# Two-layer encoder in float32 on one core: half of the Strassen weight sums of the first MLP product made by accumulating DMA, and a fourth Strassen pair in the second

## The chip, the core and the metric

The kernel runs on one core of one Trainium2 chip. The metric is the device time of one execution in microseconds; lower is better. TensorE (PE) multiplies, VectorE (DVE) and ScalarE (ACT) prepare operands and take results out of PSUM, GpSimd (POOL) and SyncE (SP) mostly issue DMAs. Each engine runs its own list of instructions in order and waits on semaphores for the others.

## The reference

Two layers over 256 tokens of width 2048, all in float32. The attention half of a layer (latent attention and neighbourhood attention, gated and merged) is untouched by the change. The part that matters is the MLP:

```python
    h = rmsnorm(x, norm_mlp[l]) @ w_ff1[l]            # 2048 -> 8192
    x = x + jnp.square(jax.nn.relu(h)) @ w_ff2[l]     # 8192 -> 2048
```

## The kernel before

**Precision.** A float32 operand is split in two: `hi` is the value cast to the PE's float32r, `lo` is the rest. A product is three matmuls (hi by hi, lo by hi, hi by lo). For weights this split is made on the core: ACT casts (`L177`), DVE subtracts (`L178`). The function `cut` does it for a whole step, in the MLP in strips 2048 columns wide.

**Tiling.** `gemm_s` computes 256 rows by 1024 columns and walks over eight steps `j` of 256 rows of the weight. A step loads one weight tile `raw` of 128 partitions by 2048 (1 MB, `L449`, on SP's queue); three such buffers exist (`RBUFS`). A plain step takes eight products, that is 24 matmuls of 512 columns. A step in `pairs` uses Strassen's scheme in Winograd's form and takes seven products, 21 matmuls, for which it needs four sums of weight blocks (`L465` makes two in one instruction, 1024 wide; `L468` and `L469` one each, 512 wide) and four sums of activation blocks (`sums_of`, `L364` to `L367`). In a Strassen step `cut` then runs over 1536 columns of the raw weights and over the 2048 columns of the four sums, where a plain step has only the 2048 raw ones. The eight products collect in eight PSUM banks; after the last step DVE combines them (eight adds at `L477`, a copy on ACT at `L478`).

**The MLP.** It runs over four blocks `b` of 2048 hidden columns. In a block two calls of `gemm_s` make the first product (`g` = 0 and 1, weights `in_w_ff1`, Strassen steps `FIRST`). Their result goes through the squared ReLU, is transposed on PE (`turned_pair`, `L398`) and split again. Two calls then make the second product (weights `in_w_ff2`, Strassen steps `SECOND`); in the last block only one, the other half being plain matmuls (`gemm_a`). So a layer has eight calls of the first kind and seven of the second. In the first three blocks the second product is added to `xt` by four accumulating DMAs a call, issued from POOL (`L870`).

**Order.** The code is written step by step, but the order in which each engine's instructions stand comes from a scheduler that runs at build time. It moves work of one step ahead of another where buffers allow. Split weights have four `hi` and four `lo` buffers in the MLP (`HBUFS`), so DVE and ACT can be about two Strassen steps ahead of PE and no more.

Of the kernel before, what the change touches and what calls it, by code (L numbers as in the profile page):

```python
# [64 lines left out]
FIRST, SECOND = (2, 4, 6), (2, 4, 6)  # L65
# [10 lines left out]
def trunk(ctx: ExitStack, tc: tile.TileContext, x, w_in, w_uq, w_ukv, rpb, w_o_mla, w_o_na,  # L76
# [36 lines left out]
    cos_sb = const.tile([P, S], F32, name="cos_sb")  # L113
    sin_sb = const.tile([P, S], F32, name="sin_sb")
    turn = const.tile([P, P], F32, name="turn")
    half = const.tile([P, 2], F32, name="half")
    mask_sb = const.tile([P, GRID_W], F32, name="mask_sb")
# [192 lines left out]
    class Norm:  # L310
# [14 lines left out]
        def scales(self):  # L325
# [5 lines left out]
            v = keep.tile([P, 2], F32, tag="var", name="var", bufs=2)  # L331
# [27 lines left out]
    def sums_of(f):  # L359
# [3 lines left out]
        s1, s2, s3, s4 = (s[:, i * P:(i + 1) * P] for i in range(4))  # L363
        nc.vector.tensor_tensor(s1, a21, a22, op=ALU.add)  # L364
        nc.vector.tensor_tensor(s2, s1, a11, op=ALU.subtract)
# [1 line left out]
        nc.vector.tensor_tensor(s3, a21, a11, op=ALU.subtract)  # L367
# [47 lines left out]
    def gemm_s(w, c0, get, order, pairs, evac):  # L415
# [31 lines left out]
        for j in order:  # L447
            raw = raws.tile([P, 2048], F32, tag="raw", name="raw", bufs=RBUFS)
            nc.sync.dma_start(raw.rearrange("p (k n) -> p k n", n=1024),  # L449
                              w[2 * j * P:(2 * j + 2) * P, c0:c0 + 1024].rearrange("(k p) n -> p k n", p=P))  # L450
# [8 lines left out]
            if strips:  # L459
                whole_ts = wpool.tile([P, 2048], F32, tag="sums", name="sums", bufs=1)  # L460
# [498 lines left out]
```

## Time and profile before

Three runs gave 2616.14, 2615.67 and 12601.07 us; the median is 2616.14.

| | us |
|---|---|
| median of the runs | 2616.14 |
| profiled execution | 2616.59 |
| its span, first to last instruction | 2614.8 |
| ACT busy | 1483.6 (57%) |
| POOL busy | 101.2 (4%) |

The chain of work that ended last is PE for 88% of the span and instruction issue for 8%; DVE has 2% and ACT 1% of it. The granted TensorE clock is 0.999 of full speed, so throttling plays no part. DMA moved 508.95 MB, 195 GB/s in the mean.

To read the rows: a group gives its line, engine, operation, tiles and shapes, the count, the busy time in us, and the mean of one in ns. The table by stretches gives for each engine its busy time and, in brackets, how many instructions. In the timeline the first number is the start and the second the length in us. A matmul's row shows its whole passage through the array, and passages overlap, so what a matmul costs is the distance between starts.

### The profile page before, as it was taken

Reading aid. Unit: us, or ns where it says so; the run is one execution under the profiler, and the core shown is the slowest. Engines: PE = TensorE matmul, PEld = TensorE weight load, DVE = VectorE, ACT = ScalarE, POOL = GpSimd, SP = SyncE. Lnnn points to the kernel's source line nnn. Section 1 sums busy time; section 2 is a strip of 40 time slices with the busy share of each in tenths; the row PEclk is TensorE's granted clock in tenths of the full one; section 3 lists DMA queues with packets and bytes.
Section 4 is the critical chain, followed back from the end, with each engine's and each line's share of the span. In section 5 each row is a group of like instructions: output and inputs, shape, how many; then the busy total and the mean of one; then the engine's idle time right before and its main releaser. Section 6 shows DMA issues by size and latency. Waiting matters only on the chain.

```text
span 2614.8 us, 32295 instructions
## 1 busy us (share of the span) xinstructions
PE 2588.5 (99%) x12450; PEld 2173.8 (83%) x12450; DVE 2183.3 (83%) x2570; ACT 1483.6 (57%) x1737; POOL 101.2 (4%) x117
## 2 busy tenths in 40 slices
PE   8999999999999999999999999999999999999998
PEld 7888888888888888888888888888888888888886
DVE  6668789789998898988667787896999988988885
ACT  6555556556655656556545555564665556565563
POOL 1100000000000010000001000000000000100000
PEclk9999999999999999999999999999999999999999
DMA  7555555555566575675555555544556766856763
GB/s 243 184 160 187 199 193 162 162 192 192 196 210 224 193 236 194 207 236 189 180 192 177 167 186 193 194 160 161 194 178 211 235 197 194 247 194 209 234 194 129
DMA packets 175257, 508.95 MB, mean 195 GB/s; under 512 B 13696, under 2 KB 18176, under 8 KB 175104
## 3 DMA queue, kind: packets, MB, share of 16 engines
q1 hardware_dynamic: 166192, 490.08, 56.5%
q0 software_dynamic: 8768, 16.78, 3.3%
q8 instruction: 97, 1.59, 0.2%
q14 instruction: 56, 0.46, 0.1%
q10 hardware_dynamic: 144, 0.04, 0.0%
HBM read 492.18 MB, written 2.10 MB: 189 GB/s over the span
## 4 chain that ended last, share of the span: by engine, by line
PE 88%; issue 8%; DVE 2%; ACT 1%; DMA 0%; POOL 0%; SPq 0%; POOLq 0%; DVEq 0%; ACTq 0%
PE bank L428 59%; PE bank L244 8%; PE bank L279 7%; PE bank L248 4%; PE bank L283 3%; PE bank L223 2%; PE bank L398 1%; PE bank L224 1%; PE bank L252 1%; PE bank L254 1%; PE bank L253 1%; DVE lo L178 1%; PE bank L559 1%; PE bank L496 0%; ACT hi L177 0%
## 5 line engine op out<-in xcount | busy, mean ns | idle before, releaser
L428 PE MATMUL bank<-hi,pair 128*128 128x512 f32 x5124 | 1284.2, 390 | 4.1 <-ACT hi L177 3.9
L428 PEld LDWEIGHTS bank<-hi,pair 128*128 128x128 f32 x5124 | 958.0, 188 | 204.8 <-ACT hi L177 5.6
L178 DVE TENSOR_TENSOR lo<-raw,hi 128x2048 fp32r<-128x2048 f32 (+3 forms) x416 | 741.8, 1796 | 77.3 <-ACT hi L177 50.9
L177 ACT CAST hi<-raw 128x2048 fp32r<-128x2048 f32 (+3 forms) x416 | 622.8, 1517 | 307.5 <-PE bank L428 163.3
L428 PE MATMUL bank<-lo,pair 128*128 128x512 f32 x2562 | 697.6, 390 | 0.0
L428 PEld LDWEIGHTS bank<-lo,pair 128*128 128x128 f32 x2562 | 479.7, 188 | 99.3
L177 ACT CAST hi<-sums 128x2048 fp32r<-128x2048 f32 (+1 forms) x150 | 244.9, 1638 | 292.3 <-DVE sums L469 167.8
L178 DVE TENSOR_TENSOR lo<-sums,hi 128x2048 fp32r<-128x2048 f32 (+1 forms) x150 | 290.8, 1947 | 98.6 <-ACT hi L177 58.7
L202 DVE TENSOR_TENSOR lo<-raw,hi 128x1024 fp32r<-128x1024 f32 (+1 forms) x224 | 269.3, 1208 | 117.2 <-ACT hi L201 116.5
L201 ACT CAST hi<-raw 128x1024 fp32r<-128x1024 f32 (+1 forms) x224 | 230.6, 1036 | 217.7 <-PE bank L279 84.7
L244 PE MATMUL bank<-hi,pair 128*128 128x512 f32 x1024 | 261.0, 391 | 0.0
L244 PEld LDWEIGHTS bank<-hi,pair 128*128 128x128 f32 x1024 | 190.3, 188 | 38.2
L477 DVE TENSOR_TENSOR wide<-wide,bank 128x512 f32<-128x512 f32 x336 | 214.9, 679 | 6.5 <-PE bank L428 6.4
L279 PE MATMUL bank<-pair,hi 128*128 128x512 f32 x768 | 203.4, 397 | 4.3 <-ACT hi L201 3.1
L465 DVE TENSOR_TENSOR sums<-raw 128x1024 f32<-128x1024 f32 x126 | 153.6, 1219 | 6.2 <-DMA raw<-in_w_ff 4.8
L279 PEld LDWEIGHTS bank<-pair,hi 128*128 128x128 f32 x768 | 136.3, 190 | 26.8 <-ACT hi L201 3.5
L248 PE MATMUL bank<-lo,pair 128*128 128x512 f32 x512 | 141.6, 391 | 0.0
L283 PEld LDWEIGHTS bank<-pair,lo 128*128 128x128 f32 x768 | 106.9, 190 | 8.7
L248 PEld LDWEIGHTS bank<-lo,pair 128*128 128x128 f32 x512 | 95.6, 188 | 19.4
L283 PE MATMUL bank<-pair,lo 128*128 128x256 f32 x768 | 111.6, 283 | 0.0
L407 ACT CAST pair<-wide 128x512 fp32r<-128x512 f32 x110 | 68.2, 620 | 56.8 <-DVE wide L366 54.5
L469 DVE TENSOR_TENSOR sums<-raw,sums 128x512 f32<-128x512 f32 x126 | 86.6, 687 | 2.1
(131 smaller groups left out, 1727.3 us busy)
## 6 DMA issues: line engine op xcount, KB each, us to landing
raw<-in_w_ff SPq DMA_DIRECT2D x256, 1024.0 KB, 5.2
raw<-in_w_in SPq DMA_DIRECT2D x124, 1024.0 KB, 5.1
raw<-in_w_out SPq DMA_DIRECT2D x32, 1024.0 KB, 5.2
raw<-in_w_o_na SPq DMA_DIRECT2D x16, 1024.0 KB, 5.0
raw<-in_w_o_mla SPq DMA_DIRECT2D x16, 1024.0 KB, 5.0
xt<-wide POOLq DMA_DIRECT2D x48, 256.0 KB, 5.5
raw<-in_w_ukv SPq DMA_DIRECT2D x8, 1024.0 KB, 5.0
raw<-in_w_uq SPq DMA_DIRECT2D x8, 768.0 KB, 4.6
```

The costliest lines, as they stand in the source:

```text
L177: nc.scalar.copy(hi, src)
L178: nc.vector.tensor_tensor(lo, src, hi.bitcast(F32), op=ALU.subtract)
L201: nc.scalar.copy(hi, src)
L202: nc.vector.tensor_tensor(lo, src, hi.bitcast(F32), op=ALU.subtract)
L244: nc.tensor.matmul(ps[t], a, wh[:, k], start=k0 + k + i == 0, stop=False)
L248: nc.tensor.matmul(ps[t], sides(have(acts, k0 + k), t)[0], wl[:, k], start=False, stop=k0 + k == nk - 1)
L279: nc.tensor.matmul(ps[m], wh[:, k, m * P:(m + 1) * P], have(acts, k0 + k), start=k0 + k == 0, stop=False)
L283: nc.tensor.matmul(ps[m][:, :S], wl[:, k, m * P:(m + 1) * P], have(acts, k0 + k)[:, :S], start=False, stop=k0 + k == nk - 1)
L428: nc.tensor.matmul(b[i], x, y, start=count[i] == 1, stop=count[i] == total[i])
L465: nc.vector.tensor_tensor(ts[0].rearrange("p (a n) -> p a n", a=2), raw[:, :512].rearrange("p (a n) -> p a n", a=1).to_broadcast([P, 2, 512]),
L469: final = nc.vector.tensor_tensor(t4, raw[:, 1536:], t2, op=ALU.subtract)
L477: add = lambda o, a, c: nc.vector.tensor_tensor(o, a, c, op=ALU.add)
```

## The change

- `SECOND` goes from steps 2, 4, 6 to steps 2, 3, 5, 6: a fourth Strassen step in every `gemm_s` call of the second product.
- In the first product (`fed=True`) the sums t1 and t3 are no longer made on DVE at `L465`. Two DMAs on SP's queue load the two blocks that are not shared straight into a new tile `t13` (two buffers); when they have landed, one accumulating DMA from POOL adds the shared block, read twice, to both. `raw` is then loaded by two smaller DMAs without that block. t2 and t4 stay on DVE.
- To make this an addition, the signs of the sums are turned round: weight sums are now all additions, activation sums and the final combination take the subtractions. `sums_of` makes two of its four sums in one instruction.
- The one `sums` tile of 2048 columns in strips becomes `t13` (two buffers) and `t24` (one), each 1024 wide, and `cut` casts and subtracts each half by itself, into one `hi` and one `lo` tile.
- To make room for the second `t13`: the rotary and mask tables live in the attention half's pool and are loaded again in the second layer, and the outputs that nobody reads of the sum-of-squares activations go into tiles that are free anyway.

```diff
-FIRST, SECOND = (2, 4, 6), (2, 4, 6)
+FIRST, SECOND = (2, 4, 6), (2, 3, 5, 6)
...
-        def cut(src):
+        def cut(src, more=None):
             out, step = [], 2048 if strips else 1024
+            if more is not None:
+                hi, lo = (wpool.tile([P, 2048], F32R, tag=tag, name=tag, bufs=hbufs) for tag in ("hi", "lo"))
+                for c, v in ((0, src), (1024, more)):
+                    cs = slice(c, c + 1024)
+                    nc.scalar.copy(hi[:, cs], v)
+                    nc.vector.tensor_tensor(lo[:, cs], v, hi[:, cs].bitcast(F32), op=ALU.subtract)
+                return [(hi[:, i:i + 512], lo[:, i:i + 512]) for i in range(0, 2048, 512)]
...
-            nc.sync.dma_start(raw.rearrange("p (k n) -> p k n", n=1024),
-                              w[2 * j * P:(2 * j + 2) * P, c0:c0 + 1024].rearrange("(k p) n -> p k n", p=P))
+            src = w[2 * j * P:(2 * j + 2) * P, c0:c0 + 1024].rearrange("(k p) n -> p k n", p=P)
+            if fed and j in pairs:
+                t13 = wpool.tile([P, 1024], F32, tag="t13", name="t13", bufs=2)
+                fore, twice = (t13.rearrange("p (a n) -> p a n", a=2), src[:, 0:1, :512].to_broadcast([P, 2, 512]))
+                nc.sync.dma_start(t13[:, :512], src[:, 0, 512:])
+                nc.sync.dma_start(t13[:, 512:], src[:, 1, :512])
+                nc.gpsimd.dma_start(fore, twice, accum_op=ALU.add)
+                nc.sync.dma_start(raw[:, 512:1024], src[:, 0, 512:])
+                nc.sync.dma_start(raw[:, 1024:], src[:, 1])
+            else:
+                nc.sync.dma_start(raw.rearrange("p (k n) -> p k n", n=1024), src)
...
-                whole_ts = wpool.tile([P, 2048], F32, tag="sums", name="sums", bufs=1)
-                ts = whole_ts[:, :1024], whole_ts[:, 1024:]
+                if not (fed and j in pairs):
+                    t13 = wpool.tile([P, 1024], F32, tag="t13", name="t13", bufs=2)
+                ts = t13, wpool.tile([P, 1024], F32, tag="t24", name="t24", bufs=1)
...
-            nc.vector.tensor_tensor(ts[0].rearrange("p (a n) -> p a n", a=2),
-                                    raw[:, :512].rearrange("p (a n) -> p a n", a=1).to_broadcast([P, 2, 512]),
-                                    raw[:, 512:1536].rearrange("p (a n) -> p a n", a=2), op=ALU.subtract)
-            nc.vector.tensor_tensor(t2, raw[:, 1024:1536], t1, op=ALU.subtract)
-            final = nc.vector.tensor_tensor(t4, raw[:, 1536:], t2, op=ALU.subtract)
+            if not fed:
+                nc.vector.tensor_tensor(ts[0].rearrange("p (a n) -> p a n", a=2),
+                                        raw[:, :512].rearrange("p (a n) -> p a n", a=1).to_broadcast([P, 2, 512]),
+                                        raw[:, 512:1536].rearrange("p (a n) -> p a n", a=2), op=ALU.add)
+            nc.vector.tensor_tensor(t2, raw[:, 1024:1536], t1, op=ALU.add)
+            final = nc.vector.tensor_tensor(t4, raw[:, 1536:], t2, op=ALU.add)
...
-            w1, w3, w2, w4 = cut(whole_ts) if strips else cut(ts[0]) + cut(ts[1])
+            w1, w3, w2, w4 = cut(*ts) if strips else cut(ts[0]) + cut(ts[1])
...
+        if l:
+            tables()
...
-                gemm_s(w_ff1[l], b * D + g * 1024, lambda j: have(xg, j), range(8), FIRST, relu2)
+                gemm_s(w_ff1[l], b * D + g * 1024, lambda j: have(xg, j), range(8), FIRST, relu2, True)
```

The scheduler sets the order anew. Three places matter for what follows. The line numbers in the rows of the changed kernel are its own.

SP's queue at the start of the first product of the second block, before (one row a weight tile, steps 0 to 4):

```order
L449 DMA raw_7126<-in_w_ff1 128x2x1024
L449 DMA raw_7160<-in_w_ff1 128x2x1024
L449 DMA raw_7190<-in_w_ff1 128x2x1024
L449 DMA raw_7229<-in_w_ff1 128x2x1024
L449 DMA raw_7259<-in_w_ff1 128x2x1024
```

The same place now (`L461` and `L462` load a `t13`, `L464` and `L465` the rest of its `raw`), steps 0 to 5 and the `t13` of steps 2, 4 and 6:

```order
L467 DMA raw_7202<-in_w_ff1 128x2x1024
L461 DMA t13_7267<-in_w_ff1 128x512
L462 DMA t13_7267<-in_w_ff1 128x512
L467 DMA raw_7236<-in_w_ff1 128x2x1024
L461 DMA t13_7342<-in_w_ff1 128x512
L462 DMA t13_7342<-in_w_ff1 128x512
L464 DMA raw_7266<-in_w_ff1 128x512
L465 DMA raw_7266<-in_w_ff1 128x1024
L467 DMA raw_7311<-in_w_ff1 128x2x1024
L464 DMA raw_7341<-in_w_ff1 128x512
L465 DMA raw_7341<-in_w_ff1 128x1024
L467 DMA raw_7382<-in_w_ff1 128x2x1024
```

The `t13` of step 2 stands ahead of the weight tile of step 1, that of step 4 ahead of the tile of step 2; that of step 6 (`t13_7413`) comes right after these rows, since it takes the buffer that step 2 frees.

POOL's queue from the end of the second block to the third, before (the accumulating DMAs into `xt` of the two calls of the second product):

```order
L870 DMA xt0_87<-wide_8064 128x512
L870 DMA xt0_87<-wide_8066 128x512
L870 DMA xt1_88<-wide_8065 128x512
L870 DMA xt1_88<-wide_8067 128x512
L870 DMA xt0_87<-wide_8344 128x512
L870 DMA xt0_87<-wide_8346 128x512
```

The same place now (`L891` is the old `L870`, `L463` the accumulating DMA into a `t13`):

```order
L891 DMA xt0_82<-wide_8198 128x512
L891 DMA xt0_82<-wide_8200 128x512
L891 DMA xt1_83<-wide_8199 128x512
L891 DMA xt1_83<-wide_8201 128x512
L463 DMA t13_8577<-in_w_ff1 128x2x512
L463 DMA t13_8652<-in_w_ff1 128x2x512
L891 DMA xt0_82<-wide_8495 128x512
L891 DMA xt0_82<-wide_8497 128x512
L891 DMA xt1_83<-wide_8496 128x512
L891 DMA xt1_83<-wide_8498 128x512
L463 DMA t13_8723<-in_w_ff1 128x2x512
```

The first two accumulations of the next block stand between the two groups for `xt`, ahead of the group that waits for the end of the second product; only that of step 6 stands behind it.

DVE in the second product of the second block, first call, from step 4 (a Strassen step) to step 5, before:

```order
L465 TENSOR_TENSOR sums_7936<-raw_7934 128x1024
L178 TENSOR_TENSOR lo_7907<-raw_7904,hi_7906 128x2048
L468 TENSOR_TENSOR sums_7936<-raw_7934,sums_7936 128x512
L364 TENSOR_TENSOR wide_7764<-wide_7762 128x128
L367 TENSOR_TENSOR wide_7764<-wide_7762 128x128
L469 TENSOR_TENSOR sums_7936<-raw_7934,sums_7936 128x512
L365 TENSOR_TENSOR wide_7764<-wide_7764,wide_7762 128x128
L408 TENSOR_TENSOR pair_7770<-wide_7762,pair_7769 128x512
L178 TENSOR_TENSOR lo_7941<-raw_7934,hi_7940 128x1536
L366 TENSOR_TENSOR wide_7764<-wide_7762,wide_7764 128x128
L408 TENSOR_TENSOR pair_7774<-wide_7764,pair_7773 128x512
L178 TENSOR_TENSOR lo_7945<-sums_7936,hi_7944 128x2048
```

The same call now at step 3 (`raw_8024`), with sums of step 5 (`raw_8092`) between; `L484`, `L487` and `L488` are the old `L465`, `L468` and `L469`, `L176` is the old `L178` and `L447` its form for a half of the sums:

```order
L487 TENSOR_TENSOR t24_8027<-raw_8024,t13_8026 128x512
L484 TENSOR_TENSOR t13_8094<-raw_8092 128x1024
L488 TENSOR_TENSOR t24_8027<-raw_8024,t24_8027 128x512
L176 TENSOR_TENSOR lo_8032<-raw_8024,hi_8031 128x1536
L447 TENSOR_TENSOR lo_8036<-t13_8026,hi_8035 128x1024
L447 TENSOR_TENSOR lo_8036<-t24_8027,hi_8035 128x1024
L409 TENSOR_TENSOR pair_7884<-wide_7881,pair_7883 128x512
L487 TENSOR_TENSOR t24_8095<-raw_8092,t13_8094 128x512
L364 TENSOR_TENSOR wide_7898<-wide_7896 128x256
L409 TENSOR_TENSOR pair_7903<-wide_7896,pair_7902 128x512
L488 TENSOR_TENSOR t24_8095<-raw_8092,t24_8095 128x512
L367 TENSOR_TENSOR wide_7898<-wide_7898,wide_7896 128x128
```

What moved: the first sum of a Strassen step now stands a whole step earlier, and the subtraction on the sums is in two halves, the first of which needs only `t13`.

More of the change, by code (lines that the diff above doesn't have):

```diff
@@ L112, in trunk @@
     nc.scalar.dma_start(g_sb, gains)
[L113 to L117, printed above, removed]
+    const.tile([P, 8], F32, name="pad")
+    table = {}
     def tables():
-        for sb, src in ((mask_sb, mask), (cos_sb, cos), (sin_sb, sin), (turn, turns), (half, halves)):
-            nc.sync.dma_start(sb, src)
+        for name, src, width in (("mask", mask, GRID_W), ("cos", cos, S), ("sin", sin, S), ("turn", turns, P),
+                                 ("half", halves, 2)):
+            table[name] = tmp.tile([P, max(width, 64)], F32, tag=name, name=name, bufs=1)[:, :width]
+            nc.sync.dma_start(table[name], src)
     xt = [const.tile([P, D], F32, name=f"xt{t}") for t in range(2)]
@@ L305, in root @@
         nc.vector.tensor_scalar(v, v, 1.0 / width, EPS, op0=ALU.mult, op1=ALU.add)
-        col = keep.tile([P, 2], F32, tag="rcol", name=name, bufs=6)
+        col = keep.tile([P, 2], F32, tag="rcol", name=name, bufs=5)
         nc.gpsimd.tensor_tensor(col, v, mhalf, op=ALU.pow)
@@ L330, in scales @@
                                  start=True, stop=True)
-            v = keep.tile([P, 2], F32, tag="var", name="var", bufs=2)
+            v = keep.tile([P, 2], F32, tag="var", name="var", bufs=1)
             nc.vector.tensor_copy(v, ps[:, 0:4:2])
@@ L340, in __init__, with add @@
             self.sums = keep.tile([P, 2, 4], F32, tag="sums", name="sums", bufs=2)
-        def add(self, t, c4):
-            junk = keep.tile([P, 512], mybir.dt.bfloat16, tag="junk", name="junk", bufs=1)
+        def add(self, t, c4, junk=None):
+            if junk is None:
+                junk = small().bitcast(mybir.dt.bfloat16)
             nc.scalar.activation(junk, xt[t][:, c4 * 512:(c4 + 1) * 512], AF.Square,
@@ L347, in scale @@
         def scale(self):
-            v = keep.tile([P, 2], F32, tag="var", name="var", bufs=2)
+            v = keep.tile([P, 2], F32, tag="var", name="var", bufs=1)
             nc.vector.tensor_reduce(v, self.sums, axis=AX.X, op=ALU.add)
@@ L354, in scales @@
             self.scale()
-            self.half = keep.tile([P, 2], F32, tag="rcol", name="half", bufs=6)
+            self.half = keep.tile([P, 2], F32, tag="rcol", name="half", bufs=5)
             nc.vector.tensor_scalar_mul(self.half, self.col, 0.5)
@@ L362, in sums_of @@
         a11, a21, a12, a22 = (f[:, i * P:(i + 1) * P] for i in range(4))
[L363 to L365 removed]
+        s3, s1, s2, s4 = (s[:, i * P:(i + 1) * P] for i in range(4))
+        nc.vector.tensor_tensor(s[:, :2 * P].rearrange("p (a n) -> p a n", a=2),
+                                f.rearrange("p (a n) -> p a n", a=4)[:, 0:4:3],
+                                a21.rearrange("p (a n) -> p a n", a=1).to_broadcast([P, 2, P]), op=ALU.subtract)
+        nc.vector.tensor_tensor(s2, s1, a11, op=ALU.add)
         nc.vector.tensor_tensor(s4, a12, s2, op=ALU.subtract)
[L367 removed]
         return s
@@ L413, in turned_pair, with gemm_s @@
         yield
-    def gemm_s(w, c0, get, order, pairs, evac):
+    def gemm_s(w, c0, get, order, pairs, evac, fed=False):
         b, count, total = {}, {}, {i: 0 for i in range(1, 9)}
@@ L528, in rope @@
         pr = abank()[:, :S]
-        nc.tensor.matmul(pr, turn, t, start=True, stop=True)
+        nc.tensor.matmul(pr, table["turn"], t, start=True, stop=True)
         u = small()
-        nc.vector.tensor_tensor(u, pr, sin_sb, op=ALU.mult)
-        nc.vector.tensor_tensor(t, t, cos_sb, op=ALU.mult)
+        nc.vector.tensor_tensor(u, pr, table["sin"], op=ALU.mult)
+        nc.vector.tensor_tensor(t, t, table["cos"], op=ALU.mult)
         nc.vector.tensor_tensor(t, t, u, op=ALU.add)
@@ L622, in put @@
                 ke[e] = pair()
-                split(ke[e], t, half[:, e:e + 1])
+                split(ke[e], t, table["half"][:, e:e + 1])
         return put
```

25 lines of the change are left out of this document (13 added, 12 removed).

## Prediction

> **What bounds the kernel now.** I read the page's busy times first, then the waits of each engine, then the timeline of PE, then busy time by stretches of the MLP.
>
> ```profile
> span 2614.8 us, 32295 instructions
> PE 2588.5 (99%) x12450; PEld 2173.8 (83%) x12450; DVE 2183.3 (83%) x2570; ACT 1483.6 (57%) x1737; POOL 101.2 (4%) x117
> ```
>
> PE is busy for 99% of the span, but a matmul's row overlaps the next, so this alone does not show that PE never waits. The waits of PE and of SP's queue do:
>
> ```profile
> PE bank L428 <- ACT hi L177: 3.9, 4, 1.1
> PE bank L279 <- ACT hi L201: 3.1, 1, 3.1
> ...
> SPq L449 <- DVE lo L178: 1438.8, 296, 14.8
> ```
>
> In all 42 calls of `gemm_s` the matmuls of L428 waited 3.9 us, in four places. SP's queue waited 1438.8 us for DVE to free a weight buffer: loads come too early, not too late. Now PE's timeline in a call of the second product:
>
> ```profile
> 2214.60 4.70 PE L428 MATMUL bank<-hi,pair 128*128 128x512 f32 x20
> 2219.14 1.07 PE L428 MATMUL bank<-lo,pair 128*128 128x512 f32 x4
> ```
>
> Twenty matmuls start over 2219.14 - 2214.60 = 4.54 us: 227 ns each. A call has 3 x 21 + 5 x 24 = 183, so 41.5 us. The stretches below are first calls of the second product in the second layer's blocks 1 and 3, then the second call of block 3 and both calls of the first product in block 4 (columns: length, PE, PEld, DVE, ACT, POOL, clock, DMA share, GB/s):
>
> ```profile
> 2007.10:2050.40 43.30, 43.30 (x200) 35.96 (x199) 38.17 (x43) 26.77 (x26) 0.00 (x0) 1.00 0.57 182
> 2176.70:2220.00 43.30, 43.30 (x200) 35.96 (x199) 37.34 (x40) 26.78 (x25) 0.00 (x0) 1.00 0.52 162
> 2220.00:2261.50 41.50, 41.50 (x184) 34.35 (x184) 38.24 (x32) 21.33 (x13) 3.52 (x4) 1.00 0.87 269
> 2261.50:2303.00 41.50, 41.50 (x184) 34.35 (x183) 36.07 (x29) 21.53 (x13) 3.50 (x4) 1.00 0.73 226
> 2303.00:2346.30 43.30, 43.30 (x200) 35.92 (x199) 38.13 (x38) 26.47 (x25) 0.00 (x0) 1.00 0.55 186
> ```
>
> Calls last 41.5 us, or 43.3 where sixteen transposes fall in: their matmuls alone. In the MLP the number of matmuls sets the time. DVE follows at 37 to 38 of 43, so it is the next in line.
>
> **The change, part by part.** The prices:
>
> ```profile
> L428 PE MATMUL bank<-hi,pair 128*128 128x512 f32 x5124 | 1284.2, 390 | 4.1 <-ACT hi L177 3.9
> L178 DVE TENSOR_TENSOR lo<-raw,hi 128x2048 fp32r<-128x2048 f32 x186 | 423.7, 2286 | 48.4 <-ACT hi L177 35.6 <-PE bank L428 12.3
> L178 DVE TENSOR_TENSOR lo<-raw,hi 128x1536 fp32r<-128x1536 f32 x102 | 178.5, 1750 | 0.0
> L178 DVE TENSOR_TENSOR lo<-raw,hi 128x1024 fp32r<-128x1024 f32 x104 | 125.1, 1221 | 28.8 <-ACT hi L177 15.4 <-PE bank L428 11.8 <-issue 1.5
> L465 DVE TENSOR_TENSOR sums<-raw 128x1024 f32<-128x1024 f32 x126 | 153.6, 1219 | 6.2 <-DMA raw<-in_w_ff 4.8
> L469 DVE TENSOR_TENSOR sums<-raw,sums 128x512 f32<-128x512 f32 x126 | 86.6, 687 | 2.1
> L177 ACT CAST hi<-sums 128x2048 fp32r<-128x2048 f32 x102 | 195.4, 1915 | 246.7 <-DVE sums L469 167.8 <-PE bank L428 78.1 <-ACT wide L815 0.5
> L177 ACT CAST hi<-raw 128x1536 fp32r<-128x1536 f32 x102 | 151.3, 1483 | 119.7 <-DMA raw<-in_w_ff 65.9 <-PE bank L428 46.6 <-DMA raw<-in_w_out 6.4
> L177 ACT CAST hi<-raw 128x1024 fp32r<-128x1024 f32 x104 | 105.6, 1052 | 87.2 <-PE bank L428 44.8 <-PE bank L244 13.2 <-issue 12.7
> ```
>
> 1. *Fourth Strassen step in the second product.* Seven calls a layer, 14 in all, each 24 - 21 = 3 matmuls fewer: 42 x 227 ns = 9.53 us, all on the path, since PE is the path. By the Trainium skill (TensorE: Matmul & The Clock Gate, "Wait — 56ns, not 53.3ns?") warm matmuls of 512 columns start 215.7 ns apart, which would make it 9.06 us; the trace has 227 and decides.
>
> 2. *What that step costs DVE and ACT.* In place of one 2286 ns subtraction DVE has 1219 + 2 x 687 + 1750 + 2 x 1221 = 6785 ns, 4.5 us more by durations. Starts overlap by about 0.08 us an instruction, so some 4.1 us of time, in each of 14 calls: 57 us. ACT's casts grow by 1483 + 2 x 1052 - 1915 = 1.7 us a call, against 43.30 - 26.78 = 16.5 us idle. On the path: nothing where DVE has that much idle time ahead of PE's need, all of it where not. The margin is smallest late in the first call, where transposes and evacuation weigh on DVE too:
>
> ```profile
> 2206.87 1.91 ACT L177 CAST hi<-sums 128x2048 fp32r<-128x2048 f32 x1 [0.49 <-PE bank L428]
> 2210.52 1.98 PE L428 MATMUL bank<-hi,pair 128*128 128x512 f32 x8
> ...
> 2027.20 2.29 DVE L178 TENSOR_TENSOR lo<-sums,hi 128x2048 fp32r<-128x2048 f32 x1 [2.51 <-ACT hi L177]
> 2030.04 0.39 PE L428 MATMUL bank<-lo,pair 128*128 128x512 f32 x1
> ...
> DVE lo L178 <- ACT hi L177: 4.1, 3, 1.7
> ```
>
> The cast ended at 2208.78 and PE used it at 2210.52 (by the program's order): 1.74 us to spare. In the first block the subtraction ended at 2029.49 and was used at 2030.04: 0.55 us. If nothing else gave way, 4.1 us more on DVE and 0.7 us less on PE leave PE waiting 4.8 - 1.74 = 3.1 us in the six first calls of later blocks and 4.8 - 0.55 = 4.2 us in the two of first blocks: 27 us. That is the upper end; the lower is 0. But DVE idles 43.30 - 37.34 = 6.0 us in that call, 4.1 of it waiting for ACT (last row, for 2176.7 to 2220). The half-wise cast lets DVE begin after 1052 ns and not 1915, and the new order fills gaps with a sum of a later step. So 4.1 us have about 6.0 us of idle time to go into, nearly full: I take 0.25 us left in each of eight calls, 2.0 us, near the lower end. In the second calls the work comes to 38.24 + 4.1 = 42.3 us by durations against 40.8, but that call also catches up what the first left, and the call behind it falls by 3 x 1219 ns = 3.7 us: 0.
>
> 3. *Sums by DMA in the first product.* 48 Strassen steps lose 1219 ns each on DVE, 58.5 us. On the path nothing, since PE did not wait there; the time pays for item 2. The price is a chain: two loads, POOL, an accumulating DMA.
>
> ```profile
> raw<-in_w_ff SPq DMA_DIRECT2D x256, 1024.0 KB, 5.2
> xt<-wide POOLq DMA_DIRECT2D x48, 256.0 KB, 5.5
> ...
> L870 POOL DMA_DIRECT2D xt<-wide x48: 852/1151/1877, 760.4 to 2436.4; - x48
> ...
> DMA to landing us min/median/max: 3.2/5.5/8.9
> ...
> 2136.33 2.28 DVE L178 TENSOR_TENSOR lo<-sums,hi 128x2048 fp32r<-128x2048 f32 x1
> 2159.06 0.69 DVE L468 TENSOR_TENSOR sums<-raw,sums 128x512 f32<-128x512 f32 x1
> ...
> 2160.56 1.91 ACT L177 CAST hi<-sums 128x2048 fp32r<-128x2048 f32 x1 [1.89 <-DVE sums L469]
> 2166.51 3.34 PE L428 MATMUL bank<-hi,pair 128*128 128x512 f32 x14
> ```
>
> The old accumulating DMAs move 256 KB from SBUF; the new one 512 KB from HBM, a kind the trace lacks. Bounds: from 5.2 + 1.2 + 5.5 = 12 us to 5.2 + 1.9 + 2 x 8.9 = 25 us for the chain. The tightest is step 6, whose buffer comes free when step 2's sums are subtracted (2138.6) and whose sum DVE needs at 2159.06: 20.5 us. SP has nothing long ahead of it there, and POOL's four `xt` DMAs stand ahead of it in one call in four only. I take 15 us, nearer the lower end, since single such DMAs landed in 3.2 to 5.5 us: hidden, 0. At 25 us it is 4.5 us late. PE takes the cast sums after six matmuls on raw weights, at 2166.51 + 6 x 0.227 = 2167.87, and they were cast at 2162.47, so 0.9 us of lead would be left, and DVE's queue behind the late sum would use it up; I price that at about 1 us in each of 16 calls, 16 us. Where the chain is early nothing is gained either, since PE does not wait there.
>
> 4. *More traffic.* One step adds 0.26 MB of plain loads and 0.52 MB of accumulation.
>
> ```profile
> q1 hardware_dynamic: 166192, 490.08, 56.5%
> q0 software_dynamic: 8768, 16.78, 3.3%
> ```
>
> All engines' time per MB: 0.565 x 2614.8 / 490.08 = 3.0 us and 0.033 x 2614.8 / 16.78 = 5.1 us. So 0.8 + 2.7 = 3.5 us a step, 10.4 a call: the first product's shares go from 0.55 to 0.79 and from 0.73 to 0.98. Two steps' loads of that call start in the call before (0.87). Full, but loads have 1438.8 us of early waiting to eat up: 0, at worst part of item 3's 16 us.
>
> 5. *The rest.* `sums_of` in three instructions, turned signs, tables loaded again at the layer's border (0.35 MB behind three weight tiles that are there already) and unread outputs in other tiles: 0 between -1 and +1, by PE's few waits outside L428.
>
> Sum: 2616.59 (profiled execution, 0.45 above the median) - 9.53 + 2.0 = 2609.1 us. I predict 2609.
>
> **The rivals.**
> - *A: DVE runs out in the second product's first calls.* For it: margins of 1.74 and 0.55 us, and the four buffers, which stop DVE from carrying the time saved in the first product across. Against: 6.0 us idle in that very call. At full price 2616.6 - 9.5 + 27 = 2634, slower than before. It decides the sign from 9.5 / 8 = 1.2 us a call on.
> - *B: the accumulating DMA is late.* For it: an unknown kind of transfer, and DMA near its limit at a block's border. Against: 20.5 us of lead. 2609 + 16 = 2625.
> - *C: PE is not the bound and DVE is.* DVE's total rises: 28 sums of 687 ns, 14 x 1750, 232 x 1221, eight more activation splits of 0.7 us, less 34 x 1219, 14 x 2286 and 102 x 2289: about +27 us, so 2643. Against it stand 3.9 us of waits. By the Trainium skill (Perfetto Trace Analysis, "Identifying the Most-Contended Engine") matmul busy time is no measure, the weight loads' share is, and the engine with the highest share is the one to relieve; that would name DVE, 2183.3 against 2173.8 us. The even 227 ns between starts speak for PE.
> - *D: nothing is given back and the new order closes old gaps too:* 2605 or below.
>
> **Chances.** Forecast (2605.5 to 2613) 0.62; A (2613 to 2634) 0.19; B 0.10; C 0.04; D 0.05. The likeliest is the forecast, so 2609. For 8 in 10 I go from 2604, nearly all of D, to 2622, which holds half of A and most of B. Faster or slower by over 2%, about what a measurement of this kernel can tell from no change, means below 2564 or above 2668. Nothing here reaches the first: 0.01. The second takes A, B and C together: 0.03. Within: 0.96.
>
> **What would show it.** PE's matmuls at L429 (old L428) number 42 fewer, still 227 ns apart, with waits under 6 us: item 1 right. Second-product calls of 40.8 us (42.6 with transposes): right; calls longer by 1 us or more, with PE waiting for ACT hi or DVE lo: A. DVE waiting for a DMA into `t13`, landings over 10 us: B. DVE's busy time near 2210 us with an unchanged span: C. I am wrong if the time is over 2613, or if calls of the first product lengthen at all.

## The result and the profile after

| | before | after |
|---|---|---|
| median of the runs, us | 2616.3 | 2637.1 |
| span of the profiled execution, us | 2614.8 | 2637.4 |
| matmuls in the 42 calls of `gemm_s` (hi rows + lo rows) | 5124 + 2562 = 7686 | 5096 + 2548 = 7644 |

The changed kernel is slower: ratio 1.008, 95% interval 1.0068 to 1.0092 (further down, too, the brackets behind a ratio are this interval). The prediction was 2609, 2604 to 2622. 42 matmuls went and the span grew by 22.6 us, so PE waits some 32 us more than before. The engines' row and the waits, of the changed kernel:

```profile
span 2637.4 us, 32886 instructions
PE 2595.5 (98%) x12408; PEld 2160.0 (82%) x12408; DVE 2196.5 (83%) x2684; ACT 1515.9 (57%) x1875; POOL 154.4 (6%) x165
...
ACT hi L175 <- DMA raw<-in_w_ff: 169.0, 72, 5.8
...
ACT hi L446 <- DVE t L488: 99.3, 58, 5.2
...
DVE t L487 <- DMA t<-in_w_ff: 44.0, 6, 8.8
...
PE bank L429 <- ACT hi L175: 7.6, 10, 1.3
PE bank L429 <- DVE wide L496: 7.0, 10, 1.2
```

PE's waits are short and many: ten for a cast of weights, ten for a bank that DVE has not yet emptied. These two rows hold 14.6 of the 32 us; PE's weight loads wait for the same two, 14.4 and 14.3 us, and these waits may overlap with the others. The long waits lie one step back. ACT waits 169.0 us for weight tiles (74.7 before), and DVE waits 44.0 us for a sum made by DMA, in just six places, one in each first call (`g` = 0) of the first product in blocks 1 to 3 of the two layers (blocks are counted from 0 here, as in the code). Four successive calls, from the second product of one block into the first product of the next (columns: length, PE, PEld, DVE, ACT, POOL, clock, DMA share, GB/s):

```profile
2192.90:2235.50 42.60, 42.60 (x197) 35.35 (x196) 40.98 (x46) 27.41 (x29) 0.00 (x0) 1.00 0.52 169
2235.50:2277.10 41.60, 41.12 (x181) 33.63 (x180) 38.39 (x37) 22.35 (x17) 4.75 (x5) 1.00 0.78 230
2277.10:2319.30 42.20, 42.13 (x185) 33.98 (x183) 32.08 (x29) 20.31 (x15) 7.26 (x8) 1.00 1.02 308
2319.30:2364.00 44.70, 43.69 (x200) 35.94 (x200) 39.24 (x42) 30.58 (x31) 2.30 (x2) 1.00 0.74 235
```

The first has the 42.6 us that its three fewer matmuls should give (43.3 - 0.68). In the third DMA is full, and DVE, relieved of its sums, works only 32 of 42 us: it waits. The fourth lasts 44.7 us where it took 43.3.

To see all calls at once I took from each trace the time between the first matmuls of successive calls, less that of the same call before, plus 0.68 us (3 x 227 ns) where a call has a fourth Strassen step. What is left is what the call lost. It is summed below over the calls of a kind, in us; "first" is the first MLP call of a layer, and in the last column, a layer's last call (taken from its first matmul to its last), some loss is an exchange with the plain matmuls that run beside it. "Feeding" is short for the sums by DMA, and a call that has them is fed.

| kernel | first (2) | 1st product, g=0 (6) | 1st product, g=1 (8) | 2nd product, g=0 (6) | 2nd product, g=1 (6) | last (2) | median, us |
|---|---|---|---|---|---|---|---|
| changed | 0.2 | 7.5 | 9.3 | 6.4 | 4.4 | 7.8 | 2637.1 |
| e1 feeding, three steps | 0.2 | 0.5 | 1.4 | 2.9 | 0.0 | -1.8 | 2621.6 |
| e2 four steps, no feeding | 10.1 | 0.0 | 0.5 | 11.7 | 0.0 | 3.2 | 2635.4 |
| e3 no accumulation | 0.2 | 2.7 | 0.3 | 3.4 | 2.7 | 5.4 | 2615.2 |
| e4 two steps of three fed | 0.9 | 10.2 | 4.5 | 19.8 | 3.1 | 6.9 | 2650.7 |
| e5 four steps in g=1, no feeding | 11.2 | 0.0 | 0.5 | 0.1 | 0.0 | 0.0 | 2626.6 |
| e6 four steps, g=1 fed | 10.4 | 2.8 | 0.2 | 3.9 | 0.6 | 5.9 | 2630.5 |
| e7 plain DMA for the accumulating | 0.2 | 0.4 | 2.1 | 6.1 | 1.4 | 8.1 | 2621.8 |
| e8 four steps in g=1, all fed | 0.2 | 0.1 | 2.9 | 8.0 | 0.0 | 6.3 | 2631.4 |
| e9 before, four steps in g=1 | 0.0 | 0.0 | -0.1 | 0.9 | 1.8 | -1.8 | 2615.1 |
| e10 as e5, first call fed | 0.2 | 0.0 | 0.3 | 0.0 | 0.0 | 0.1 | 2614.7 |
| e11 as e6, block 0 fed too | 0.2 | 2.9 | 0.3 | 4.1 | 2.8 | 5.5 | 2618.9 |
| e12 no `xt` DMA from g=1 | 0.2 | 8.6 | 4.5 | 3.3 | 1.1 | 6.0 | 2630.4 |
| e13 four steps in g=0, all fed | 0.2 | 0.5 | 5.6 | 3.5 | 0.5 | 7.0 | 2626.0 |

### The profile page after: what moved, and what is told of

Same layout as the page of the kernel before. It is cut to its first block, busy times and chain, and to the rows that moved or that the text cites. A ratio compares the mean times of both kernels' runs of the same rounds, so it can differ in the third digit from the quotient of the medians.

```text
span 2637.4 us, 32886 instructions
## 1 busy us (share of the span) xinstructions
PE 2595.5 (98%) x12408; PEld 2160.0 (82%) x12408; DVE 2196.5 (83%) x2684; ACT 1515.9 (57%) x1875; POOL 154.4 (6%) x165
## 4 chain that ended last, share of the span: by engine, by line
PE 66%; DMA 13%; DVE 12%; issue 7%; ACT 1%; SPq 0%; POOL 0%; DVEq 0%; POOLq 0%; ACTq 0%
PE bank L429 37%; DMA raw<-in_w_ff 9%; PE bank L242 8%; PE bank L277 7%; DVE lo L176 6%; DMA t<-in_w_ff 4%; PE bank L246 4%; PE bank L281 3%; DVE lo L447 2%; PE bank L221 2%; DVE wide L496 1%; PE bank L399 1%; PE bank L222 1%; DVE t L487 1%; PE bank L250 1%
## 5 line engine op out<-in xcount | busy, mean ns | idle before, releaser
L429 PE MATMUL bank<-hi,pair 128*128 128x512 f32 x5096 | 1303.2, 391 | 17.4 <-ACT hi L175 7.6
L429 PEld LDWEIGHTS bank<-hi,pair 128*128 128x128 f32 x5096 | 949.7, 188 | 234.2 <-ACT hi L175 14.4
L175 ACT CAST hi<-raw 128x2048 fp32r<-128x2048 f32 (+3 forms) x416 | 615.1, 1501 | 364.4 <-DMA raw<-in_w_ff 169.0
L176 DVE TENSOR_TENSOR lo<-raw,hi 128x2048 fp32r<-128x2048 f32 (+3 forms) x416 | 733.6, 1778 | 61.1 <-ACT hi L175 43.2
L429 PE MATMUL bank<-lo,pair 128*128 128x512 f32 x2548 | 716.3, 391 | 1.1 <-DVE lo L447 0.8
L446 ACT CAST hi<-t 128x1024 fp32r<-128x1024 f32 x232 | 239.6, 1049 | 186.1 <-DVE t L488 99.3
L447 DVE TENSOR_TENSOR lo<-t,hi 128x1024 fp32r<-128x1024 f32 x232 | 276.4, 1219 | 16.2 <-PE bank L429 14.5
L242 PE MATMUL bank<-hi,pair 128*128 128x512 f32 x1024 | 261.7, 391 | 0.0
L496 DVE TENSOR_TENSOR wide<-wide,bank 128x512 f32<-128x512 f32 x252 | 165.5, 680 | 7.5 <-PE bank L429 7.4
L246 PE MATMUL bank<-lo,pair 128*128 128x512 f32 x512 | 143.3, 391 | 0.0
L463 POOL DMA_DIRECT2D t<-in_w_ff x48 | 58.2, 1212 | 1277.6 <-DMA t<-in_w_ff 680.2
L487 DVE TENSOR_TENSOR t<-raw,t 128x512 f32<-128x512 f32 x116 | 79.6, 686 | 63.5 <-DMA t<-in_w_ff 44.0
L484 DVE TENSOR_TENSOR t<-raw 128x1024 f32<-128x1024 f32 x68 | 83.1, 1223 | 30.9 <-DMA raw<-in_w_ff 30.6
```

The lines of the kernel that those rows point to most:

```text
L175: nc.scalar.copy(hi, src)
L176: nc.vector.tensor_tensor(lo, src, hi.bitcast(F32), op=ALU.subtract)
L242: nc.tensor.matmul(ps[t], a, wh[:, k], start=k0 + k + i == 0, stop=False)
L246: nc.tensor.matmul(ps[t], sides(have(acts, k0 + k), t)[0], wl[:, k], start=False, stop=k0 + k == nk - 1)
L429: nc.tensor.matmul(b[i], x, y, start=count[i] == 1, stop=count[i] == total[i])
L446: nc.scalar.copy(hi[:, cs], v)
```

## The experiments

Each starts from the changed kernel, but for e9. T1 and T2 in the first expectations are two theories: the loss comes from the DMA side, or from the fourth step's lack of time on DVE and ACT.

**e1, feeding alone.**

```diff
-FIRST, SECOND = (2, 4, 6), (2, 3, 5, 6)
+FIRST, SECOND = (2, 4, 6), (2, 4, 6)
```

> The changed kernel with three Strassen steps in the second product (2, 4, 6) as before; the sums by DMA in the first product stay. 42 matmuls more than the changed kernel. Theory T1, the loss comes from the DMA side (DMA engines full in the first product, the chain of step 6 late, the lateness handed on): the loss stays without the fourth step, about 2616 + 15 = 2628 to 2634 us. Theory T2, the loss comes from the fourth step, for which DVE and ACT have no room in the second product: 2614 to 2619 us, no slower than the kernel before.

2621.6 us, ratio 1.0016 (1.0007 to 1.0026), between the ranges of the two theories. The sums by DMA, together with the small edits of item 5, cost 5 us without the fourth step, although DMA is nearly as full as in the changed kernel (shares of 0.95 to 1.00 in the first calls of blocks 1 to 3, against 0.99 to 1.03). The three calls across a border:

```profile
1098.40:1139.80 41.40, 41.40 (x184) 34.32 (x183) 36.75 (x33) 23.23 (x18) 5.95 (x6) 1.00 0.97 295
1139.80:1181.30 41.50, 41.50 (x184) 34.36 (x183) 32.62 (x30) 20.33 (x16) 7.22 (x7) 1.00 0.97 283
1181.30:1224.60 43.30, 43.30 (x200) 35.93 (x199) 36.84 (x39) 27.80 (x29) 1.21 (x1) 1.00 0.68 213
```

PE is busy throughout. A nearly full DMA alone does not stop it. The other difference to the changed kernel is in the first row: 0.97 against 0.78, that is, loads for the next block run early.

**e2, the fourth step alone.**

```diff
-                gemm_s(w_ff1[l], b * D + g * 1024, lambda j: have(xg, j), range(8), FIRST, relu2, True)
+                gemm_s(w_ff1[l], b * D + g * 1024, lambda j: have(xg, j), range(8), FIRST, relu2)
```

> The changed kernel with all sums of the first product back on DVE (no feeding by DMA); the fourth step in the second product stays. T1: the first product goes back to 41.5 and 43.3 us a call, and only small losses are left in the second: 2607 to 2613 us. T2: DVE has 58 us more work than in the changed kernel and as little room in the second product, so the calls of the second product lose 1.2 us or more each: 2622 us or more.

2635.4 us, ratio 1.007 (1.0055 to 1.0085), in T2's range, with no accumulation into a `t13` anywhere. But all second calls take 40.8 us and so lose nothing, against T2; the first calls of the second product lose 11.7 us and the last ones 3.2. DVE and PE in such a first call:

```profile
1080.21 1.22 DVE L484 TENSOR_TENSOR t<-raw 128x1024 f32<-128x1024 f32 x1 [0.33 <-DMA raw<-in_w_ff]
1081.35 2.28 DVE L176 TENSOR_TENSOR lo<-raw,hi 128x2048 fp32r<-128x2048 f32 x1
...
1083.69 2.11 PE L429 MATMUL bank<-lo,pair 128*128 128x512 f32 x8 [0.74 <-DVE lo L176]
```

PE starts when the subtraction of 1081.35 ends. Ahead of that stood the first sum of a step that comes later, which itself waited 0.33 us for its load. Idle time of DVE was there, but not ahead of the work that was late. This is one wait of 0.74 us; that the others are of the same kind is not shown. The other 10 us, in a layer's first MLP call, are taken up in e5.

**e3, without the accumulating DMA; `t13` is used as loaded.**

```diff
-                nc.gpsimd.dma_start(fore, twice, accum_op=ALU.add)
```

> The changed kernel without the accumulating DMA: t13 is loaded and used as it is, so the shared block is left out of t1 and t3. PE, DVE and ACT do the same instructions; 25 MB of accumulating traffic and the second half of the chain are gone. T1: the DMA share in the first calls falls from about 1.0 to about 0.8, the first product is at 41.5 and 43.3 us a call again: 2607 to 2613 us. T2: nothing changes in the second product; what goes is at most the lengthening of the first product's calls: 2618 to 2628 us.

2615.2 us, ratio 0.9996 (0.9987 to 1.0006): between the two. Against the changed kernel 22 us, so that is the price of the accumulation beside four steps; e1 has it at 5 at most beside three. Against e2, 20 us less: DVE's relief is worth something, half of it in a layer's first call. The first calls of the second product lose 3.4 us in place of 11.7.

**e4, steps 2 and 4 fed, step 6 summed on DVE.**

```diff
+            by_dma = fed and j in pairs and j != 6
...
-            if fed and j in pairs:
+            if by_dma:
...
-                if not (fed and j in pairs):
+                if not by_dma:
...
-            if not fed:
+            if not by_dma:
```

> The changed kernel with steps 2 and 4 of the first product fed by DMA and step 6 back on DVE; four Strassen steps in the second product stay. T1: a third of the added traffic goes, and with it the step whose chain comes last; the first product loses less than half of what it loses now: 2612 to 2622 us. T2: DVE has 20 us more work, the second product loses what it lost: 2632 to 2642 us.

2650.7 us, ratio 1.0129 (1.0114 to 1.0144): worse than either theory has it. The late `t13` of step 6 is gone, but a weight tile is late in its place. The same two lines (`L487` and `L484` there) wait 18.2 and 30.6 us in the changed kernel; in e4:

```profile
DVE t L488 <- DMA raw<-in_w_ff: 49.3, 12, 6.6
DVE t L485 <- DMA raw<-in_w_ff: 41.8, 53, 1.8
```

So step 6's accumulation into the recycled `t13` buffer is not needed for a loss of this size. DMA is still at 1.00 to 1.02 in those calls. That the first calls of the second product lose 19.8 us was not taken apart further: the scheduler gave this kernel an order of its own.

**e5, the fourth step only in the second calls, no feeding** (with e2's edit).

```diff
-                gemm_s(w2, g * 1024, lambda j: have(hid, j), range(8), SECOND, residual2)
+                gemm_s(w2, g * 1024, lambda j: have(hid, j), range(8), SECOND if g else (2, 3, 6), residual2)
```

> No feeding; the fourth Strassen step stands only in the second calls of the second product (steps 2, 3, 5, 6), the first calls have three (2, 3, 6): 6 x 3 matmuls fewer than before, 18 x 227 ns = 4.1 us. In the run with pairs alone all six second calls lasted 40.80 us, so they lost nothing, and the first calls lost 1.3 to 3.1 us each. Theory 'the fourth step fits where no transposes and no evacuation of the first product fall in': 2616.6 - 4.1 = 2612.5, so 2611 to 2614.5, second calls 40.8 us, first calls 43.3. Rival 'the second calls only pass their lack of DVE time on': 2615 to 2622, with first-product calls or first calls of the second product longer than before.

2626.6 us, ratio 1.0038 (1.0025 to 1.0051), above both ranges. Of 30 MLP calls 28 lose next to nothing, as the theory says; all of the loss, 11.2 us, is in the first MLP call of each layer, where neither theory had it. DVE and PE there:

```profile
645.36 1.22 DVE L447 TENSOR_TENSOR lo<-t,hi 128x1024 fp32r<-128x1024 f32 x1
646.50 2.29 DVE L176 TENSOR_TENSOR lo<-raw,hi 128x2048 fp32r<-128x2048 f32 x1
648.70 1.22 DVE L484 TENSOR_TENSOR t<-raw 128x1024 f32<-128x1024 f32 x1
649.83 0.29 DVE L368 TENSOR_TENSOR wide<-wide 128x128 f32<-128x128 f32 x1
...
650.15 0.62 ACT L408 CAST pair<-wide 128x512 fp32r<-128x512 f32 x1 [3.44 <-DVE wide L368]
...
650.82 0.50 PE L429 MATMUL bank<-hi,pair 128*128 128x512 f32 x1 [3.33 <-ACT pair L408]
```

An activation sum of 0.29 us stands behind 4.7 us of weight work (1.22 + 2.29 + 1.22); ACT waits for it and PE for ACT. That is the order, not a lack of time. The 3.3 us are followed by a slower clock (last section).

**e6, four steps; only the second calls of the first product fed** (`relu2, g == 1)` for `relu2, True)`).

> Four Strassen steps in the second product as in the changed kernel; sums by DMA only in the second call of the first product. Theory 'DMA is full in the first call of the first product, because weight buffers come free late in the call before and the accumulations fall on top': the 7.5 us lost in those calls and most of the 4.4 us lost in the calls before go, DMA share there 0.75 to 0.9 instead of 1.0: 2622 to 2629. Rival 'every accumulating DMA costs its own delay on the chain wherever it stands': half of the 21 us that the accumulation costs goes, but DVE has half of its relief less, which gives about 5 us back: 2629 to 2635. Rival 'DVE's total decides': 2634 to 2638.

2630.5 us, ratio 1.005 (1.0034 to 1.0066), in the first rival's range, but 10.4 us of it is e5's stall, since the layer's first call is not fed either. Without it some 2620, below the first theory's range. The calls after it do as the first theory says: 0.2 us lost in g=1 in place of 9.3, 2.8 in g=0 in place of 7.5.

**e7, a plain DMA in place of the accumulating one, same queue, tile and waits.**

```diff
-                nc.gpsimd.dma_start(fore, twice, accum_op=ALU.add)
+                nc.gpsimd.dma_start(fore, twice)
```

> The changed kernel with a plain DMA in place of the accumulating one, same queue, same source, same tile, same waits: t13 then holds the shared block twice, so t1 and t3 lack the other block. The chain of two loads, POOL, DMA stays; only the kind of the transfer changes (by the profile of before 3.0 us of all engines per MB in place of 5.1, so 0.52 x 2.1 = 1.1 us a step, 3.3 us a call). Theory 'the accumulation's traffic costs the time': 2618 to 2627. Rival 'the length of the chain costs it': 2632 to 2638, within 5 us of the changed kernel.

2621.8 us, ratio 1.0021 (1.0012 to 1.0031), in the range of the traffic theory: the kind of the transfer is worth 15 us. A plain transfer with the same chain costs 6.6 us against e3. Rows of e7, then of the changed kernel:

```profile
q0 software_dynamic: 15680, 41.95, 5.9%
t<-in_w_ff POOLq DMA_DIRECT2D x48, 512.0 KB, 6.0
```

```profile
q0 software_dynamic: 21824, 41.95, 8.8%
t<-in_w_ff POOLq DMA_DIRECT2D x48, 512.0 KB, 9.2
```

Same bytes, 77 us less time of all engines (0.088 x 2637.4 - 0.059 x 2620.3), and 3.2 us less from issue to landing. The chain is shorter too, and DVE waits 27.0 us for `t13` in place of 44.0, so this run does not tell traffic from length.

**e8, all of the first product fed, the fourth step only in the second calls** (e5's edit alone).

> Sums by DMA in the whole first product; the fourth Strassen step only in the second calls of the second product (18 matmuls fewer than before). Theory 'DVE lacks time in the first calls alone': feeding alone took 2621.6, so 2621.6 - 4.1 = 2617.5, 2616 to 2619.5. Rival 'the fourth step in the second call holds the weight buffers longer, so that the loads of the next first product start late and meet the accumulations': second calls move 230 GB/s instead of 295 and first-product calls lose 1 to 2 us each: 2622 to 2630.

2631.4 us, ratio 1.0057 (1.0041 to 1.0073), above both ranges: 18 matmuls fewer than e1 and 9.8 us slower. The second calls take 40.8 us and lose nothing themselves; they move 256 to 259 GB/s, between the rival's 230 and 295. DVE waits 42.1 us for `t13`, again in six places, all in first calls of the first product. These lose 0.1 us, and the loss shows in later calls: 2.9, 8.0 and 6.3 us.

**e9, the kernel before with e5's edit of the steps and `SECOND` = 2, 3, 5, 6; e10, e5 with only the first MLP call of a layer fed** (`b == g == 0` for `True`).

> The kernel before (its sums, its tiles, no feeding) with a fourth Strassen step in the second calls of the second product alone (steps 2, 3, 5, 6 there, steps 2, 3, 6 in the first calls): 18 matmuls fewer, 4.1 us. Theory 'the fourth step fits into the second calls, and the 5 us lost in the first MLP call of a layer in three runs come from the order that the changed code got there': 2612.5, 2611 to 2614, all second calls 40.8 us, first MLP call of a layer 44.0 us. Rival 'the loss in a layer's first MLP call comes with the fourth step's activation sums': 2620 to 2625, that call 49 us.

> Fourth step in the second calls only, sums by DMA only in the very first MLP call of each layer (3 of 48 sums a layer... 6 in all). Theory 'that call stalls 5 us because DVE's sums stand ahead of an activation sum that PE waits for': with the sums off DVE there the call is back at 44.1 us, and 2626.6 less 11.2 gives 2615.4: 2613.5 to 2617. Rival 'the stall moves to another call': 2620 to 2628.

2615.1 us, ratio 0.9992 (0.9983 to 1.0001), and 2614.7, ratio 0.999 (0.9981 to 1.0). e10 is back at 44.1 us in the layer's first call, so e5's stall is the order around DVE's sums there; e9 never had it, so it does not come with the fourth step. e10 lies in its range, e9 1 us above its own. Both are some 2 us above the 2612.5 that 18 matmuls fewer would give: e9 loses 0.9 us twice in second calls, and in e10 the stretches outside the MLP are 1.5 and 1.0 us longer. These are the best versions, about 2 us under the kernel before (2616.9 beside them), at the edge of what the runs can tell.

**e11, four steps, fed everywhere except in the first calls (g = 0) of blocks 1 to 3** (`g == 1 or b == 0` for `True`).

> Four Strassen steps in all calls of the second product; sums by DMA everywhere in the first product except in the first calls (g = 0) of blocks 1 to 3, where the `xt` accumulations and the tail of the second product meet them. Theory 'the loss needs the accumulations in just those calls, since DVE enters them late and the sum of step 6 then comes behind its need': 2637.1 less 18 to 13 us, 2618 to 2624, no wait of DVE on a DMA into t13 over 2 us. Rival 'the loss is spread over all calls with accumulations': 36 of 48 sums remain, so 2630 to 2636.

2618.9 us, ratio 1.0007 (0.9998 to 1.0016), as the theory has it. (Six calls hold 18 of the 48 fed steps, so 30 remain, not the 36 that the rival counts; the rival's sum would then lie near 2637.1 - 18/48 x 22 = 2629, still far off.) Not feeding these six calls gives back 18 of the 28 us by which the prediction missed. DVE no longer waits for `t13` at all. The border of the same block as in e1, now:

```profile
1093.50:1136.00 42.50, 41.90 (x181) 33.48 (x180) 38.75 (x37) 22.19 (x17) 3.50 (x4) 1.00 0.72 217
1136.00:1178.30 42.30, 42.09 (x185) 34.20 (x184) 38.63 (x35) 22.97 (x17) 5.87 (x6) 1.00 0.92 292
1178.30:1221.60 43.30, 43.30 (x200) 35.96 (x199) 38.73 (x43) 28.47 (x29) 1.22 (x1) 1.00 0.73 225
```

**e12, without the accumulating DMAs into `xt` from the second calls of blocks 0 to 2.**

```diff
+                            if b < NB - 1 and g:
+                                continue
                             if b < NB - 1:
```

> The changed kernel without the accumulating DMAs into xt from the second calls of blocks 0 to 2 (that half of the second product is not added). This takes 1 MB of accumulation, by the profile of before 5.1 us of all DMA engines, out of each first call of the first product, and four issues off POOL's queue ahead of the sum of step 6; the chain of that sum (buffer free, two loads, POOL, accumulation) stays. Theory 'DMA is full there, traffic sets the pace': DMA share there 0.85 to 0.9, 2620 to 2628. Rival 'the buffer of step 6 comes free too late and the chain is too long': DVE still waits 4 us or more for that sum in each of the six calls, 2630 to 2637.

2630.4 us, ratio 1.0051 (1.0037 to 1.0064), at the lower edge of the rival, yet not for its reason. The wait for `t13` is down, and the wait for weight tiles is up:

```profile
DVE t L487 <- DMA raw<-in_w_ff: 46.2, 14, 6.1
...
DVE t L487 <- DMA t<-in_w_ff: 7.2, 4, 3.4
```

The DMA share there is 0.93 to 0.97, not 0.87, and the core still moves some 300 GB/s in those calls, as in the changed kernel: plain loads took the place of what was left out.

**e13, all of the first product fed, the fourth step only in the first calls** (`(2, 3, 6) if g else SECOND`).

> Sums by DMA in the whole first product as in the changed kernel; the fourth Strassen step only in the first calls of the second product (and the single call of the last block), three in the second calls: 24 matmuls fewer than before, 5.4 us. Theory 'with four steps in the second call DVE has no time to get ahead of PE before the next block begins, and only that lead hid the accumulations': with three steps there it gets ahead again, first calls of the first product last 41.5 us, DVE waits under 10 us in all for a DMA into t13, second-call DMA share 0.95 as with feeding alone; feeding alone 2621.6 less 5.4 plus 0 to 6 us of the loss in the first calls gives 2616 to 2622. Rival 'full DMA is enough, lead or not': the first product's calls lose 1 to 2 us each as in the changed kernel, 2628 to 2634.

2626.0 us, ratio 1.0036 (1.0022 to 1.005), between the two. The first calls of the first product are whole again (0.5 us lost), as the theory says, but so are e8's (0.1), which have four steps ahead of them. The calls after them still lose 5.6 us, and DVE still waits 34.9 us for `t13`, not the 10 at most of the theory.

## Why the prediction was wrong

**What failed first: item 3, the 20.5 us of lead, from which "hidden, 0" follows.** It weighs most, since 22 of the 28 us go with the accumulation (e3). The lead is the time from step 2's buffer coming free to DVE needing step 6's sum. It was called the tightest, but it was read in a second call of the first product (g = 1, from 2133.4). All six waits came in first calls (g = 0), and these had less already in the profile before. DVE in the one from 2091.9:

```profile
2096.94 2.28 DVE L178 TENSOR_TENSOR lo<-sums,hi 128x2048 fp32r<-128x2048 f32 x1
...
2112.59 0.69 DVE L468 TENSOR_TENSOR sums<-raw,sums 128x512 f32<-128x512 f32 x1
```

The buffer comes free at 2099.22, 7.3 us into the call, and step 6's sum begins at 2112.59: a lead of 13.4 us, in all six of these calls 13.4 to 13.5. That is less than the 15 us that item 3 took for the chain. POOL's four `xt` DMAs stand ahead of the sum in these same calls, six of 16 and not one in four. The chain of step 6's sum in the changed kernel, call from 1144.9, in rows of SP, POOL and DVE:

```profile
1157.96 0.33 SPq L461 DMA_DIRECT2D t<-in_w_ff  x1
1158.34 1.11 SPq L462 DMA_DIRECT2D t<-in_w_ff  x1
...
1167.13 1.21 POOL L463 DMA_DIRECT2D t<-in_w_ff  x1 [5.43 <-ACT hi L175]
...
1177.24 0.69 DVE L487 TENSOR_TENSOR t<-raw,t 128x512 f32<-128x512 f32 x1 [7.43 <-DMA t<-in_w_ff]
```

The third row names ACT, but POOL waits there for the two loads above it, which landed by 1166.55. The buffer comes free 13.1 us into the call, and DVE is ready for the sum at 1177.24 - 7.43 = 1169.81, that is 11.9 us later. The lead was 11.9 us and the chain 19.2, to its landing. The same in the six calls of four kernels:

| | chain starts, us into the call | lasts | DVE idle ahead of the sum |
|---|---|---|---|
| changed | 10.0 to 13.1 | 17.7 to 20.5 | 5.9 to 8.8 |
| e8 (fourth step in g=1) | 8.6 to 10.3 | 17.8 to 19.5 | 6.0 to 7.7 |
| e13 (fourth step in g=0) | 6.1 to 7.7 | 17.4 to 19.4 | 4.9 to 6.6 |
| e1 (three steps) | 4.0 to 5.7 | 10.9 to 20.3 | 0 to 5.1 |

The chain lies within the 12 to 25 us given, above the 15 taken, and above the lead in all calls but some of e1's. In e1 that hardly costs PE anything: DVE waits there too, up to 5.1 us, but the sum lands 15 to 24.5 us into the call, where the changed kernel has 27.7 to 32.2. What moved with the fourth step is the chain's start: in the second calls the step fills DVE (item 2 had 42.3 of 40.8 us and priced it at 0), so DVE comes into the next block 5 us later than in e1 (e8), and 2 us more come from the first calls (e13). e9 shows the same without feeding: step 2's buffer comes free 11.1 to 11.7 us into these calls, 7.2 to 7.3 in the kernel before. So item 3 had its lead from the wrong kind of call, item 2 used up the time by which DVE was ahead of PE, and each was priced as if the other part had not been made. The call's own length did not show it: 40.8 us, right, in e2, e5 and e8.

**Item 3, "the time pays for item 2".** Of 58.5 us taken off DVE, 44.0 came back as the wait for `t13`. While DVE stands there it frees no weight tile, so SP loads none (in the call from 1144.9 it issues nothing from 1170.2 to 1180.3), and all engines after it begin the next call behind. In the profile that is PE waiting for `wide L496`: DVE empties the banks late.

**Item 4, "full, but ...: 0".** The shares were right (0.98 forecast, 0.99 to 1.03 measured in blocks 1 to 3; 0.79 and 0.74 to 0.81). The 1438.8 us by which SP came early did not help: most of it is still there (1200.2 and 166.5 us of waiting for DVE at `L467` and `L464`), spread over all calls, and SP can only be early where buffers are free. With DMA full a weight tile takes longer to land: in the changed kernel's call from 1144.9, and then before, from 2091.9 (last number, median us):

```profile
raw<-in_w_ff SPq DMA_DIRECT2D x6, 1024.0 KB, 7.8
```

```profile
raw<-in_w_ff SPq DMA_DIRECT2D x8, 1024.0 KB, 4.8
```

In e1's call at the same place (from 1139.8) such tiles take 8.2 us, and PE does not wait, so slow landings alone do not make the loss; something of the fourth step has to come to it, by the table the late start. That the loss needs the accumulations in those six calls is shown (e11), and that 15 of its 22 us (e3) come with their kind (e7). How much is traffic and how much the length and late start of the chain stays open: e7 shortens the chain along with the traffic, e11 takes both away, in e13 the chain still starts 2 us later than in e1, and in e12 other loads fill the place of the traffic taken away.

**Item 2, the size.** The mechanism was the one given. Taken were 2.0 us, the upper end was 27; e2, where DVE keeps all its sums, has 11.7 + 3.2 = 15, and e3, relieved of them, still has 3.4 us in the first calls. The failed step is "4.1 us have about 6.0 us of idle time to go into": DVE's idle time there lay behind loads and casts, and in the wait shown under e2 the order put a sum of a later step ahead of the split that PE waited for, where I had counted such a sum as filling a gap.

**Item 1** was right, 42 matmuls and 40.8 us where nothing waits. **Item 5**, 0 with 1 us either way, is at its upper end or above: e5 and e10 have all of its edits, and their stretches outside the MLP are together 0.9 and 2.5 us longer than before. Of e1's 5 us, 1.4 are lost in each first call of the second product in block 0; e5 and e10 lose nothing there, and the cause is open. Two slips change no term: the stretches that the prediction puts in blocks 1, 3 and 4 lie in the layer's first, second and third block, and the terms of rival C add up to 26 us, not 27.

**The rivals.** A and B both came true, A at half its price (15 of 27), B above it (22 for 16). They were given as alternatives, and the range reached half of A and most of B alone. Together they make 2616.3 - 9.5 + 15 + 22 = 2644; the changed kernel is 7 us better, since A is smaller there: its first calls of the second product lose 6.4 us in place of e2's 11.7. C did not come true: DVE's total grew by 13 us, and in e5, with 2225.1 us of DVE, 28 calls are within 0.15 us of the shortest they can be.

## What to carry to other kernels

A lead that hides a transfer has to be read in every kind of call: here it was 20.5 us in one kind and 13.4 in the kind that mattered. It is also a quantity of the schedule before, and a change that fills the engine which builds it up, one stage earlier, uses it up without lengthening that stage: price such pairs of edits together. Idle time of an engine counts as cover only if it lies ahead of the work that is late; look up in the order what stands before that work. With DMA near 1.0 and three buffers, a long wait of the consumer also stops the loads.

## What the runs showed of the hardware

An accumulating DMA of 512 KB took 9.2 us from issue to landing, a plain one of the same bytes from the same queue 6.0 (e7 and changed kernel). Subtracting what this queue cost before (3.3% of 2614.8 us), the 25.17 MB into `t13` cost (232.1 - 86.3) / 25.17 = 5.8 us of all engines per MB accumulating and (154.6 - 86.3) / 25.17 = 2.7 plain.

A stall can be dearer than its length. In e5 PE resumed at 650.82 after the 3.3 us, and then matmuls started 427 ns apart for a while. Two stretches of e5:

```profile
652.55:655.15 2.60, 2.60 (x8) 2.02 (x7) 2.55 (x7) 2.44 (x3) 0.00 (x0) 0.50 0.24 90
655.30:660.00 4.70, 4.70 (x22) 3.84 (x21) 2.81 (x3) 1.84 (x4) 0.00 (x0) 0.98 0.40 111
```

The granted clock was 0.50 from 652.1 to 655.5, beginning 1.3 us after PE was back at work, which adds about 1.6 us to the stall (8 x 0.2). The Trainium skill (TensorE: Matmul & The Clock Gate, "HAM oscillation — how this bites in real kernels") warns of idle gaps over some 3.4 us; e5's gap of 3.33 us lies at that figure. But e4 shows the same half clock (0.50 in 746.9 to 749.2) after a wait of 1.61 us and a second of 0.35, so here it also followed shorter gaps. It did not always: the same two waits in e4's second layer, 1.61 and 0.35 us up to 2058.2, were followed by a clock of 1.00.
